# Two bias loads of a mixture-of-experts kernel, moved to GpSimd behind the first weight load

## The chip, the cores and the metric

The kernel runs on one core of one Trainium2 chip. That core has five instruction streams: TensorE (PE in the profile), VectorE (DVE), ScalarE (ACT), GpSimd (POOL) and SyncE (SP). Any of ACT, POOL and SP can issue a DMA; the bytes are moved by the 16 DMA engines of the core. The metric is the device time of one execution in microseconds, lower is better.

## The reference: what is computed

There are 8 experts. Each has its own 256 rows of 512 inputs, a first weight matrix of 512 x 2048, a second of 2048 x 512, and two biases:

```
h   = np.matmul(x, w1) + b1[:, np.newaxis, :]
h   = np.maximum(h, 0)
out = np.matmul(h, w2) + b2[:, np.newaxis, :]
```

Everything comes in and goes out as float32. The inputs are x (8 x 256 x 512), w1 (8 x 512 x 2048), w2 (8 x 2048 x 512), b1 (8 x 2048, that is 64 KB) and b2 (8 x 512, that is 16 KB). Each w1[e] and each w2[e] is 4 MB in HBM.

## The kernel before

The kernel is written by hand for each engine inside one critical section, with semaphores for the order. Weights are cast from float32 to float16 while they are loaded, which only DMAs issued by GpSimd do here, so one GpSimd DMA per matrix brings 4 MB from HBM into 2 MB of SBUF (the last two w2 come in two halves). There are three buffers for w1 and three for w2 (`NW = 3`).

Steps. A loop over s = 0 to 10 runs on every engine (`E + LAG` steps, `LAG = 3`). In step s TensorE does the first layer of expert s (64 matmuls with 128 x 128 weights in 16 groups of four, tile `ph`, line 297) and then the second layer of expert s - 3 (tile `po`, two bias matmuls of line 324 and 32 matmuls of line 314). So steps 0 to 2 have only a first layer, and steps 8 to 10 only a second.

VectorE turns x of the next expert into `xT` by 32 x 32 block transposes (lines 124 and 127) and evicts one half of `po`. ScalarE takes each group of `ph` out of PSUM with the bias b1 and the relu into `hT` (line 231), and evicts the other half of `po` (line 211). There are four PSUM buffers for `ph` (`NPH = 4`): TensorE may be at most four groups ahead of ScalarE, which counts free buffers on the semaphore `s_credit`.

Bias b1. ScalarE needs b1 as one column per group and expert, with the 128 hidden rows on partitions. In the kernel before, b1 is loaded ahead of the section by a DMA of ScalarE (lines 132 and 133) as 32 rows of 2 KB into `b1_rows`; VectorE turns it with four 32 x 512 transposes (line 196) after the x of expert 0, and then raises `s_b1`, for which ScalarE waits once (line 221).

Bias b2. It is loaded by GpSimd right behind the first w1 (line 178), as one row of 4096 numbers cast to float16, in one partition, behind three rows that no result uses. The matmuls of line 324 put it into `po` at the start of each second layer: the weights are a row of ones, the moving operand is 512 numbers at `s * H`.

Order of GpSimd's DMAs (all in one queue, q0): after the semaphore `s_first` (raised by ScalarE's first instruction) come w1 of expert 0, b2, w1 of 1, x of 2 and 3, w1 of 2. From then on each w1 waits until the first layer three experts back is done (`s_ph`, line 154), and each w2 from expert 3 on waits for the second layer three back (`s_po`, line 162). At the end it stores the results of experts 0 to 3 and 4 to 5 (`flush`).

SyncE loads x of experts 0 and 1 (line 135), and then is the gate for TensorE: in each step it waits for `xT` and for the landing of the matrices, and raises `s_go` (lines 246 and 247). In step 0, ahead of these, it waits for b2 (lines 254 and 255). It stores the results of the last two experts.

Of the kernel before, what the change touches and what calls it, by code (L numbers as in the profile page):

```python
# [10 lines left out]
def kernel(  # L11
# [12 lines left out]
    nc = tc.nc  # L24
    fp32 = mybir.dt.float32
    fp16 = mybir.dt.float16
    relu = mybir.ActivationFunctionType.Relu
    PE = mybir.EngineType.PE
    E, T, H = x.shape
    M = w1.shape[2]  # L30
    P = 128
    nTB = T // P
    nKC = H // P
    nJ = M // P
    half = nJ // 2
    TURN = half - 1
    B = 32
    nB = P // B
    LAG = 3
    NW = 3  # L40
    NPH = 4
# [6 lines left out]
    def sbuf(name, shape, dtype):  # L48
        return ctx.enter_context(nc.sbuf_tensor(name, shape, dtype))

    def sem(name):
        return ctx.enter_context(nc.semaphore(name=name))


    ones1 = sbuf("ones1", [1, P], fp16)
    warm = sbuf("warm", [1, P], fp16)
    b2_sb = sbuf("b2_sb", [1, (LAG + E) * H], fp16)
    b1_rows = sbuf("b1_rows", [E * nB, M // nB], fp32)
    b1T = sbuf("b1T", [P, nJ * B + nB - 1], fp32)
    w1_sb = sbuf("w1_sb", [P, NW * nKC * M], fp16)  # L60
    w2_sb = sbuf("w2_sb", [P, NW * nJ * H], fp16)
    xT = sbuf("xT", [P, 2 * nKC * T], fp16)
    hT = sbuf("hT", [P, (LAG + 1) * nJ * T], fp16)
    x32 = [sbuf(f"x32_{e}", [P, nTB, H], fp32) for e in range(2)]
# [19 lines left out]
    landed = {}  # L84

    def load(engine, key, **kw):
        landed[key] = sem(f"d_{key}")
        engine.dma_start(**kw).then_inc(landed[key], 16)  # L88

    s_b1 = sem("b1T")  # L90
# [16 lines left out]
    def transposes(e):  # L107
# [21 lines left out]

    nc.vector.memset(ones1[:], 1.0)  # L130
    tc.keep_in_program_order(nc.scalar.activation(out=warm[:], in_=ones1[:], func=relu).then_inc(s_first, 1))  # L131
    tc.keep_in_program_order(nc.scalar.dma_start(
        out=b1_rows[:], in_=b1.rearrange("e (b i) -> (e b) i", b=nB)))
    for e in range(2):
        tc.keep_in_program_order(nc.sync.dma_start(
            out=x32[e][:], in_=x[e].rearrange("(p tb) h -> p tb h", tb=nTB)))
# [15 lines left out]
    def load_w1(e):  # L152
        if e >= NW:
            nc.gpsimd.wait_ge(s_ph, nJ * (e - NW + 1))
        at = e % NW * nKC * M
        load(nc.gpsimd, f"w1_{e}",
             out=w1_sb[:, at : at + nKC * M].rearrange("p (kc m) -> p kc m", kc=nKC),
             in_=w1[e].rearrange("(p kc) m -> p kc m", kc=nKC))

    def load_w2(e):  # L160
        if e >= NW:
            nc.gpsimd.wait_ge(s_po, nTB * (e - NW + 1))
        dst = w2_sb[:, e % NW * nJ * H : (e % NW + 1) * nJ * H].rearrange("p (j h) -> p j h", j=nJ)
        src = w2[e].rearrange("(p j) h -> p j h", j=nJ)
        cuts = (0, half, nJ) if e in HALVED else (0, nJ)
        for lo, hi in zip(cuts, cuts[1:]):
            load(nc.gpsimd, f"w2_{e}_{lo}", out=dst[:, lo:hi], in_=src[:, lo:hi])

    def flush(first):
        n = GROUPS[first]  # L170
        for tb in range(nTB):
# [3 lines left out]

    nc.gpsimd.wait_ge(s_first, 1)
    load_w1(0)
    load(nc.gpsimd, "b2", out=b2_sb[:, LAG * H :],
         in_=b2.rearrange("e h -> (e h)").rearrange("(o f) -> o f", o=1))
    for s in range(1, E + LAG - 1):  # L180
        if s < E:
            if s in X_LOADS:
                load_x(s)
            load_w1(s)
        if s >= LAG:
            load_w2(s - LAG)
    load_w2(E - 1)
# [4 lines left out]

    nc.vector.sem_inc(s_last, -16 * len(HALVED))
    nc.vector.sem_inc(s_xT, 1)
    for b in range(nB):
        turned = nc.vector.transpose(  # L196
            out=b1T[b * B : (b + 1) * B, nB - 1 - b : nB - 1 - b + nJ * B],
            in_=b1_rows[:].rearrange("r (i j) -> r j i", j=nJ),
        )
    turned.then_inc(s_b1, 1)  # L200

# [16 lines left out]
        if s >= LAG:  # L218
            evict(s - LAG, 1)

    nc.scalar.wait_ge(s_b1, 1)
    for s in range(E + LAG):
        if s < E:
            split = group_of.get(s, (s, 1))[1]
            if s > LAG:
                nc.scalar.wait_ge(s_po, nTB * (s - LAG))
            for j in range(nJ):
                mine = hT[:, s % (LAG + 1) * nJ * T : (s % (LAG + 1) + 1) * nJ * T]
                bias_at = j * B + s * nB + nB - 1
                nc.scalar.wait_ge(s_ph, nJ * s + j + 1)  # L230
                nc.scalar.activation(  # L231
                    out=mine.rearrange("p (tb j k i) -> p j tb k i", tb=nTB, j=nJ, k=split)[:, j],
                    in_=ph[:, j % NPH, 0:T].rearrange("p (tb i k) -> p tb k i", tb=nTB, k=split),
                    func=relu,
                    bias=b1T[:, bias_at : bias_at + 1],
                    scale=1.0,
                ).then_inc(s_credit, 1)
        if s >= LAG:
            evict(s - LAG, 0)
# [5 lines left out]
    def go(key, n=1):  # L245
        nc.sync.wait_ge(landed[key], 16)  # L246
        nc.sync.sem_inc(s_go, n)  # L247

    def store(e, p0, p1, engine):
        dst = out[e].rearrange("(p r) h -> p r h", r=nTB)  # L250
        engine.dma_start(out=dst[p0:p1], in_=results[e][p0:p1]).then_inc(s_last, 16)

    for s in range(E + LAG):
        if s == 0:
            nc.sync.wait_ge(landed["b2"], 16)
        if s < E:
            nc.sync.wait_ge(s_xT, s + 1)
            go(f"w1_{s}")
        e = s - LAG
        if e >= 2:  # L260
            for tb in range(nTB):
                nc.sync.wait_ge(s_out[tb], e - 1)
        if e >= 0 and e not in HALVED:
            go(f"w2_{e}_0", 2)
        elif e == E - 2:
            go(f"w2_{e}_0")
            go(f"w2_{e}_{half}")
        elif e == E - 1:
            go(f"w2_{e}_0")
            for tb in range(nTB):  # L270
                nc.sync.wait_ge(s_out[tb], e)
            store(E - 2, 0, P, nc.sync)
            go(f"w2_{e}_{half}")
# [13 lines left out]
    with nc.Fori(0, E + LAG, 1, engines=[PE]) as s:  # L287
        nc.tensor.wait_ge(s_credit, NPH)
        w_at = at(s % NW * (nKC * M), (NW - 1) * nKC * M)
        with nc.tensor.If(s < E):  # L290
            x_at = at(s % 2 * (nKC * T), nKC * T)
            take(s_go)
            with nc.Fori(w_at, w_at + nJ, half, engines=[PE]) as w_from:
                w_from = w_from.with_bounds(min_val=0, max_val=(NW - 1) * nKC * M + half)
                for j in range(half):
                    for kc in range(nKC):
                        last = nc.tensor.matmul(  # L297
                            ph[:, j % NPH, 0:T],
                            w1_sb[:, bass.ds(w_from + (kc * M + j), P, nJ)],
                            xT[:, bass.ds(x_at + kc * T, T)],  # L300
                            start=(kc == 0),
                            stop=(kc == nKC - 1),
                        )
                        if kc == 0:
                            last.wait_op(s_credit, j + 1, "sem-ge")
                    last.then_inc(s_ph, 1)
                nc.tensor.sem_inc(s_credit, -half)
        with nc.tensor.If(s >= LAG):
            h_at = at((s + 1) % (LAG + 1) * (nJ * T), LAG * nJ * T)
            bank_at = at((s + 1) % 2 * (nTB * H), nTB * H)  # L310
            banks = [po[:, bass.ds(bank_at + tb * H, H)] for tb in range(nTB)]

            def second(tb, h_from, w2_from, j, stop=False):
                return nc.tensor.matmul(  # L314
                    banks[tb],
                    hT[:, bass.ds(h_from + (tb * nJ + j) * P, P)],
                    w2_sb[:, bass.ds(w2_from + j * H, H)],
                    start=False,
                    stop=stop,
                )  # L320

            nc.tensor.wait_ge(s_go, 1)
            for tb in range(nTB):
                nc.tensor.matmul(banks[tb], ones1[:], b2_sb[:, bass.ds(s * H, H)], start=True, stop=False)  # L324
            with nc.Fori(h_at, h_at + 2 * TURN * P, TURN * P, engines=[PE]) as h_from:
                h_from = h_from.with_bounds(min_val=0, max_val=LAG * nJ * T + TURN * P)
                w2_from = at((h_from - h_at) * (H // P) + w_at, ((NW - 1) * nJ + TURN) * H)
                nc.tensor.wait_ge(s_go, 1)
                for tb in range(nTB):
                    for j in range(TURN):  # L330
                        second(tb, h_from, w2_from, j)
                nc.tensor.sem_inc(s_go, -1)
            for tb in range(nTB):
                for j in range(2 * TURN, nJ):
                    last = second(tb, h_at, w_at, j, stop=(j == nJ - 1))
                last.then_inc(s_po, 1)
# [35 lines left out]
```

## Time and profile before

| what | value |
|---|---|
| median of 3 runs | 180.83 us (180.82 to 181.06) |
| the profiled execution itself | 181.16 us |
| its span, first to last instruction | 179.4 us |
| mean granted TensorE clock | 0.969 |
| PE, DVE, ACT, POOL busy | 135.3, 86.8, 75.5, 12.6 us |
| moved by DMA | 40.46 MB as counted by the profile, 226 GB/s |

In the groups of instructions a line shows the source line, the engine, the operation, what is written and from what, the shape, how often, the busy time and the mean duration. "SPq" or "PEq" is the instruction queue (the sequencer) of an engine. "us to landing" of a DMA is the time from its issue until all of its data have arrived. In the rows of the timeline the first number is the start in us, the second how long the group took; in square brackets stands the idle time of the engine ahead of it and what ended it. In the row of the slices each digit is the busy share of one fortieth of the span, in tenths.

### The profile page before, as it was taken

How to read it: one execution, taken by the hardware profiler on the slowest of the kernel's cores; microseconds unless marked ns; L12 is line 12 of the kernel's file. 1: busy time of each engine (PE TensorE's matmuls, PEld its weight loads, DVE VectorE, ACT ScalarE, POOL GpSimd, SP SyncE). 2: the span in 40 equal slices, each digit the busy share in tenths (PEclk: the TensorE clock that was granted, in tenths of full speed). 3: DMA queues.
4: the chain of work that ended last, by engine and by line, in shares of the span. 5: the costliest groups of instructions: out<-in, count | busy, mean ns of one | idle time of the engine just before them, and what ended most of it. 6: DMA issues, size and time to landing. Idle time of an engine off the chain costs nothing. (4 is left out here: it accounts for less than half of the span.)

```text
span 179.4 us, 3015 instructions
## 1 busy us (share of the span) xinstructions
PE 135.3 (75%) x784; PEld 93.1 (52%) x784; DVE 86.8 (48%) x124; ACT 75.5 (42%) x153; POOL 12.6 (7%) x27
## 2 busy tenths in 40 slices
PE   0004978868699890898978896889698896999980
PEld 0003878858689330794468543874298332434330
DVE  1989938576000299998089906992320002030110
ACT  3201686757687113483087506780487211020110
POOL 4200012020200100001010001000200003010000
PEclk9999999999999997599999999999999998799999
DMA  5999999998999999999899999999989999999995
GB/s 214 269 205 206 234 205 206 230 227 186 236 227 190 227 230 216 197 230 227 186 234 230 205 208 230 216 197 230 227 190 230 230 192 217 208 223 212 343 406 248
DMA packets 3826, 40.46 MB, mean 226 GB/s; under 512 B 448, under 2 KB 464, under 8 KB 1136
## 3 DMA queue, kind: packets, MB, share of 16 engines
q0 software_dynamic: 3200, 38.28, 96.6%
q1 hardware_dynamic: 576, 2.10, 3.0%
q10 hardware_dynamic: 48, 0.07, 0.1%
q14 instruction: 2, 0.02, 0.0%
HBM read 71.39 MB, written 4.19 MB: 421 GB/s over the span
## 5 line engine op out<-in xcount | busy, mean ns | idle before, releaser
L297 PE MATMUL ph<-xT,w_sb 128*128 x512 | 72.5, 303 | 33.2 <-PEq L282 30.3
L297 PEld LDWEIGHTS ph<-xT,w_sb 128*128 x512 | 66.6, 146 | 40.1 <-issue 29.3
L231 ACT ACTIVATE hT<-ph,b1T 128x256 f16<-128x256 f32 x128 | 60.1, 474 | 33.7 <-PE ph L297 30.0
L127 DVE STREAM_TRANSPOSE xT<-x 32x256 f16<-32x256 f16 (+1 forms) x64 | 52.7, 892 | 25.3 <-DMA x<-in_x_dram 22.0
L314 PE MATMUL po<-w_sb,hT 128*128 x256 | 58.3, 388 | 1.6 <-issue 1.6
L314 PEld LDWEIGHTS po<-w_sb,hT 128*128 x256 | 25.2, 99 | 33.9 <-issue 8.0
L211 DVE COPY out<-po 32x512 f32<-32x512 f32 (+1 forms) x20 | 13.7, 687 | 44.6 <-PE po L314 44.4
L211 ACT COPY out<-po 32x512 f32<-32x512 f32 (+1 forms) x20 | 11.5, 577 | 47.7 <-PE po L314 47.5
L88 POOL DMA_DIRECT2D w_sb<-in_w_dram x18 | 9.7, 544 | 137.4 <-PE po L314 71.2
L124 DVE STREAM_TRANSPOSE xT<-x 32x256 f16<-32x256 f16 x32 | 14.0, 436 | 0.5
L324 PE MATMUL po<-b_sb,ones 1*128 x16 | 4.8, 379 | 3.9 <-issue 2.5
L211 DVE COPY x<-po 128x512 f32<-128x512 f32 x2 | 1.4, 692 | 13.0 <-PE po L314 13.0
L211 ACT COPY x<-po 128x512 f32<-128x512 f32 x2 | 1.2, 585 | 13.3 <-PE po L314 13.3
L324 PEld LDWEIGHTS po<-b_sb,ones 1*128 1x128 f16 x16 | 1.3, 91 | 6.4 <-issue 6.1
L196 DVE STREAM_TRANSPOSE b1T<-b_rows 32x512 f32<-32x512 f32 x4 | 4.1, 1024 | 0.5 <-issue 0.5
L139 ACT CAST x<-x 128x1024 f16<-128x1024 f32 x1 | 1.0, 1045 | 3.3 <-DMA x<-in_x_dram 3.3
L137 DVE CAST x<-x 128x1024 f16<-128x1024 f32 x1 | 0.7, 724 | 3.1 <-DMA x<-in_x_dram 3.1
L88 POOL DMA_DIRECT2D out_dram<-out x2 | 1.1, 536 | 11.2 <-DVE out L211 11.2
L131 ACT ACT_TABLE_LOAD x1 | 1.3, 1283 | 0.7 <-PEq L356 0.7
L88 POOL DMA_DIRECT2D x<-in_x_dram x2 | 1.2, 608 | 0.0
L130 DVE MEMSET ones<- 1x128 f16 x1 | 0.2, 165 | 0.9 <-PEq L356 0.9
L88 POOL DMA_DIRECT2D b_sb<-in_b_dram x1 | 0.5, 507 | 0.0
(5 smaller groups left out, 0.7 us busy)
## 6 DMA issues: line engine op xcount, KB each, us to landing
w_sb<-in_w_dram POOLq DMA_DIRECT2D x14, 2048.0 KB, 41.2
w_sb<-in_w_dram POOLq DMA_DIRECT2D x4, 1024.0 KB, 22.5
out_dram<-out POOLq DMA_DIRECT2D x1, 2048.0 KB, 25.0
x<-in_x_dram SPq DMA_DIRECT2D x2, 512.0 KB, 3.9
x<-in_x_dram POOLq DMA_DIRECT2D x1, 1024.0 KB, 34.5
out_dram<-out POOLq DMA_DIRECT2D x1, 1024.0 KB, 16.4
out_dram<-x SPq DMA_DIRECT2D x2, 512.0 KB, 6.3
x<-in_x_dram POOLq DMA_DIRECT2D x1, 512.0 KB, 23.1
```

Source lines behind the costliest of these rows:

```text
L88: engine.dma_start(**kw).then_inc(landed[key], 16)
L124: last = nc.vector.transpose(out=dst[:, :, g, :, 0, :], in_=block[:, :, :, 0, :])
L127: last = nc.vector.transpose(out=dst[:, tb, g], in_=block[:, tb])
L131: tc.keep_in_program_order(nc.scalar.activation(out=warm[:], in_=ones1[:], func=relu).then_inc(s_first, 1))
L137: nc.vector.tensor_copy(out=x16[0][0][:], in_=x32[0][:])
L139: tc.keep_in_program_order(nc.scalar.copy(out=x16[1][0][:], in_=x32[1][:]))
L196: turned = nc.vector.transpose(out=b1T[b * B : (b + 1) * B, nB - 1 - b : nB - 1 - b + nJ * B], in_=b1_rows[:].rearrange("r (i j) -> r j i" ...
L211: last = copy(out=results[e][at : at + rows, k * nTB + tb, :], in_=po[k * rows : (k + 1) * rows, bank : bank + H])
L231: nc.scalar.activation(out=mine.rearrange("p (tb j k i) -> p j tb k i", tb=nTB, j=nJ, k=split)[:, j], in_=ph[:, j % NPH, 0:T].rearrange("p ...
L297: last = nc.tensor.matmul(ph[:, j % NPH, 0:T], w1_sb[:, bass.ds(w_from + (kc * M + j), P, nJ)], xT[:, bass.ds(x_at + kc * T, T)], start=(k ...
L314: return nc.tensor.matmul(banks[tb], hT[:, bass.ds(h_from + (tb * nJ + j) * P, P)], w2_sb[:, bass.ds(w2_from + j * H, H)], start=False, st ...
L324: nc.tensor.matmul(banks[tb], ones1[:], b2_sb[:, bass.ds(s * H, H)], start=True, stop=False)
```

## The change

b1 is no longer loaded by ScalarE ahead of the section. GpSimd zeroes a tile `b1_rows` of 32 rows of 2048 numbers, waits for that, and loads b1 into its first eight rows, one row of 8 KB per expert. This stands behind w1 of expert 0 and b2, and ahead of w1 of expert 1. VectorE waits for that load ahead of its four transposes, which have the same shape as before (32 x 512), now from four column ranges of the rows. The columns of `b1T` are arranged anew, and ScalarE waits for the second count of `s_b1`, since the zeroing gives the first.

b2 keeps its place in GpSimd's queue, but lands as eight rows of 512 numbers, each followed by a gap of 32 numbers in SBUF (`B2 = H + B`); the matmuls of line 324 step by `B2`. SyncE waits for b2 in step 3, where the first second layer stands, and not in step 0.

```diff
+    B2 = H + B
...
-    b2_sb = sbuf("b2_sb", [1, (LAG + E) * H], fp16)
-    b1_rows = sbuf("b1_rows", [E * nB, M // nB], fp32)
-    b1T = sbuf("b1T", [P, nJ * B + nB - 1], fp32)
+    b2_sb = sbuf("b2_sb", [1, (LAG + E) * B2], fp16)
+    b1_rows = sbuf("b1_rows", [B, M], fp32)
+    b1T = sbuf("b1T", [P, nJ * B], fp32)
...
-    tc.keep_in_program_order(nc.scalar.dma_start(
-        out=b1_rows[:], in_=b1.rearrange("e (b i) -> (e b) i", b=nB)))
...
     load_w1(0)
-    load(nc.gpsimd, "b2", out=b2_sb[:, LAG * H :],
-         in_=b2.rearrange("e h -> (e h)").rearrange("(o f) -> o f", o=1))
+    load(nc.gpsimd, "b2", out=b2_sb[:, LAG * B2 :].rearrange("o (e h) -> o e h", e=E)[:, :, 0:H],
+         in_=b2.rearrange("(o e) h -> o e h", o=1))
+    nc.gpsimd.memset(b1_rows[:], 0.0).then_inc(s_b1, 1)
+    nc.gpsimd.wait_ge(s_b1, 1)
+    load(nc.gpsimd, "b1", out=b1_rows[0:E], in_=b1)
...
+    nc.vector.wait_ge(landed["b1"], 16)
     for b in range(nB):
         turned = nc.vector.transpose(
-            out=b1T[b * B : (b + 1) * B, nB - 1 - b : nB - 1 - b + nJ * B],
-            in_=b1_rows[:].rearrange("r (i j) -> r j i", j=nJ),
+            out=b1T[b * B : (b + 1) * B],
+            in_=b1_rows[:, b * (M // nB) : (b + 1) * (M // nB)].rearrange("r (i j) -> r j i", j=nJ),
...
-    nc.scalar.wait_ge(s_b1, 1)
+    nc.scalar.wait_ge(s_b1, 2)
...
-                bias_at = j * B + s * nB + nB - 1
+                bias_at = j * B + s
...
-        if s == 0:
+        if s == LAG:
             nc.sync.wait_ge(landed["b2"], 16)
...
-                nc.tensor.matmul(banks[tb], ones1[:], b2_sb[:, bass.ds(s * H, H)], start=True, stop=False)
+                nc.tensor.matmul(banks[tb], ones1[:], b2_sb[:, bass.ds(s * B2, H)], start=True, stop=False)
```

## The prediction

> **What bounds the kernel now.** I read the slices and the DMA queues of the page first.
>
> ```profile
> span 179.4 us, 3015 instructions
> ...
> PEclk9999999999999997599999999999999998799999
> DMA  5999999998999999999899999999989999999995
> ...
> q0 software_dynamic: 3200, 38.28, 96.6%
> q1 hardware_dynamic: 576, 2.10, 3.0%
> q10 hardware_dynamic: 48, 0.07, 0.1%
> ```
>
> The DMA row shows 8 or 9 tenths in all slices but the first and the last, and the queues' shares add up to 99.7% of 16 engines' span. So the 16 DMA engines are full from the start to the end; what counts is how many engine-microseconds are queued, whether they are spread evenly, and whether an engine ever runs dry. q0 are GpSimd's DMAs, q1 SyncE's, q10 the one DMA of ScalarE, which is b1.
>
> Next, the pieces of the chain that ended last (start, duration).
>
> ```profile
> 109.46 39.44 DMA w_sb<-in_w_dram
> ...
> 149.30 0.60 PE po L324 x2
> ...
> 150.15 8.77 PE po L314 x32
> 158.92 0.53 PE po L324 x2
> 159.45 7.01 PE po L314 x32
> 166.46 0.53 PE po L324 x2
> 167.00 7.03 PE po L314 x32
> ...
> 174.05 0.69 DVE x L211
> ```
>
> The end hangs on a w2 that was issued at 109.46 and landed at 148.90: it stood 39 us in the queue. Behind it come three second layers without a break (the first takes 8.77 instead of 7.0 us because the clock row shows a 7 and an 8 there), an eviction and the last store. So two things set the end: when that w2 lands, and the DMA work left behind it.
>
> Third, how deep the queue is: the issues and their time to landing, each from the DMA view of a short window (columns: the tile, queue, count, KB, us to landing), and the timeline of the start. The first fence has, in this order, b1, w1 of expert 0, b2, w1 of 1, x of 2 and 3, w1 of 2, and w1 of 4.
>
> ```profile
> b_rows<-in_b_dram ACTq DMA_DIRECT2D x1, 64.0 KB, 3.4
> ...
> w_sb<-in_w_dram POOLq DMA_DIRECT2D x1, 2048.0 KB, 12.6
> ...
> b_sb<-in_b_dram POOLq DMA_DIRECT2D x1, 8.0 KB, 12.1
> ...
> w_sb<-in_w_dram POOLq DMA_DIRECT2D x1, 2048.0 KB, 21.3
> ...
> x<-in_x_dram POOLq DMA_DIRECT2D x1, 512.0 KB, 23.1
> ...
> w_sb<-in_w_dram POOLq DMA_DIRECT2D x1, 2048.0 KB, 32.5
> ...
> w_sb<-in_w_dram POOLq DMA_DIRECT2D x1, 2048.0 KB, 34.4
> ```
>
> ```profile
> 0.35 0.10 POOL L356 MEMSET const-uint8-127<- 128x1 uint8 x1
> 0.74 1.28 ACT L131 ACT_TABLE_LOAD   x1 [0.74 <-PEq L356]
> ...
> 1.12 0.41 ACTq L132 DMA_DIRECT2D b_rows<-in_b_dram  x1
> 2.03 0.31 ACT L131 ACTIVATE warm<-ones 1x128 f16<-1x128 f16 x1
> 2.65 0.67 POOL L88 DMA_DIRECT2D w_sb<-in_w_dram  x1 [2.21 <-ACT warm L131]
> 3.31 0.51 POOL L88 DMA_DIRECT2D b_sb<-in_b_dram  x1
> 3.80 0.58 POOL L88 DMA_DIRECT2D w_sb<-in_w_dram  x1
> ...
> 4.36 0.66 POOL L88 DMA_DIRECT2D x<-in_x_dram  x1
> ...
> 5.00 0.55 POOL L88 DMA_DIRECT2D w_sb<-in_w_dram  x1
> ...
> 12.60 4.14 DVE L196 STREAM_TRANSPOSE b1T<-b_rows 32x512 f32<-32x512 f32 x4 [0.49 <-issue]
> ...
> 16.08 9.85 PE L297 MATMUL ph<-xT,w_sb 128*128 x64 [16.08 <-PEq L282]
> 16.77 7.20 DVE L124 STREAM_TRANSPOSE xT<-x 32x256 f16<-32x256 f16 x16
> 17.22 0.47 ACT L231 ACTIVATE hT<-ph,b1T 128x256 f16<-128x256 f32 x1 [10.55 <-PE ph L297]
> 18.02 0.47 ACT L231 ACTIVATE hT<-ph,b1T 128x256 f16<-128x256 f32 x1 [0.32 <-PE ph L297]
> ...
> 21.43 5.01 ACT L231 ACTIVATE hT<-ph,b1T 128x256 f16<-128x256 f32 x11 [0.38 <-PE ph L297]
> 26.22 1.07 POOL L88 DMA_DIRECT2D w_sb<-in_w_dram  x2 [20.67 <-PE ph L297]
> ...
> 27.45 4.38 PE L297 MATMUL ph<-xT,w_sb 128*128 x32 [1.52 <-PEq L282]
> ...
> 38.30 4.35 PE L297 MATMUL ph<-xT,w_sb 128*128 x32 [1.56 <-PEq L282]
> ```
>
> Landings: w1 of 0 at 2.65 + 12.6 = 15.25, b2 at 3.31 + 12.1 = 15.4, w1 of 1 at 25.1, x of 2 at 27.5, w1 of 2 at 5.00 + 32.5 = 37.5. When w1 of 3 is issued at 26.22, the engines still have 11 us of work; from there on the queue only gets deeper (the 39 us above).
>
> **The change part by part.**
>
> *b1 out of q10 and into q0.* The bytes stay the same. q10's 0.1% of 179.4 us is about 0.18 us on every engine; finer, q1 spends 3.0% x 179.4 = 5.4 us per engine on 2.10 MB, so 64 KB (0.066 MB) spread over 16 engines cost 0.17 us on each. That leaves the queue ahead of w1 of 0, so w1 can start up to 0.17 us earlier (or not at all earlier, if its own descriptors are late: it is issued only at 2.65). In exchange the same bytes come behind b2. Every DMA of before gave its bytes to all engines as far as the shares show. Eight rows of 8 KB can hardly sit on more than eight engines unless a row is cut. Cut over 16 the net is 0; on eight engines each of those gets 0.34 us, net +0.17, and the other eight -0.17; with w1 starting no earlier, +0.34 and 0. A load has landed only when its slowest engine is done, so what counts is whether the slowest engine is among the eight. Ends: -0.17 and +0.34; I take +0.1, near the middle, since nothing in the page tells the engines apart.
>
> [...] No row of before shows a DMA of eight rows. [...]
>
> *b2 as eight rows.* 8 KB as before, in the same place. Its landing lies 0.16 us behind w1's; if half of the engines carry it, at most another 0.1 us on those. I take 0.
>
> *Zeroing b1_rows, and GpSimd's queue.* 2048 numbers per partition. The trace has no such memset on POOL: the nearest row is 0.10 us for one number. VectorE's transposes take 4.14/4 = 1.03 us for 512 numbers, so 2048 cost 4.1 us at that rate; I take 3 and bound it at 0.1 and 8 (twice that). With the wait and one more issue of 0.51 us, w1 of 1 goes out at 3.80 + 3 + 0.5 = 7.3 instead of 3.80 (bounds 4.4 and 12.3), and x of 2 and w1 of 2 behind it move alike. The engines are busy with w1 of 0 until 15.25, so this is hidden with 3 to 11 us to spare; if that cover were gone, every us of lateness would be a us of the end. Value 0.
>
> *ScalarE without its DMA issue.* 0.41 us at 1.12, under the table load that ends at 2.02; the warm-up activation that frees GpSimd waits for that load. 0.
>
> *SyncE's wait for b2.* In step 0 SyncE waits for b2, `xT` and w1. Without b2, TensorE can start 0.16 us earlier (15.25 against 15.4), at about 15.9. In step 3 the wait falls on a DMA that landed some 30 us before, and nothing queued behind it on SyncE is held. 0 at the end.
>
> *VectorE's and ScalarE's wait for b1.* This is the real move. b1's transposes can begin only when b1 has landed behind w1 of 0 and b2: about 15.4 + 0.4 = 15.8, against 12.60. They end at 15.8 + 4.14 = 19.95, and ScalarE's first activation starts at about 20.2 instead of 17.22. TensorE has four buffers: from 15.9 it does four groups at 0.85 us (the spacing of the activations, 17.22 to 18.02 and on) until 19.3, then stalls until ScalarE has freed one at 20.7. The remaining twelve groups cost 12 x 0.85 = 10.2 us at the slow pace of the start and 12 x 0.45 = 5.4 at the pace behind 21.43 (5.01 us for 11). So the first layer of expert 0 ends between 26.1 and 30.9 instead of 25.93; with about five more slow groups I take 28.5, +2.6 us. Behind it on VectorE, x of expert 1 is turned from 20.0 to 27.2 (7.20 us) instead of until 23.97, which is no later than TensorE is free. Step 1 then starts at about 30.0 instead of 27.45, and steps 1 to 3 are late by some 2.5 us. GpSimd's w1 of 3 goes out near 28.8 (at most 31.2) instead of 26.22, with the engines fed until 37.5. Cover there: 6 us or more.
>
> Where does the lateness end? Here.
>
> ```profile
> 59.78 7.08 PE L314 MATMUL po<-w_sb,hT 128*128 x32 [0.28 <-issue]
> ...
> 72.22 4.03 PE L297 MATMUL ph<-xT,w_sb 128*128 x18 [5.36 <-PEq L282]
> ...
> 37.03 1.07 POOL L88 DMA_DIRECT2D w_sb<-in_w_dram  x2 [9.21 <-PE ph L297]
> ...
> 140.81 7.08 PE L314 MATMUL po<-w_sb,hT 128*128 x32 [0.28 <-issue]
> ```
>
> Before step 4 TensorE idles 5.36 us until w1 of 4 lands (37.03 + 34.4 = 71.4). A lateness of 2.6 us, or of 5.0 at the worst pace, is swallowed there, and from 72 us on TensorE runs as before. Without that gap the 2.6 us would reach the end. Value 0.
>
> [...]
>
> *Sum.* 0.1 + 0 = +0.1 us on the profiled span, 179.5; the profiled execution took 181.16 with 1.8 us around the span, 0.3 above the median. Against the median of 180.83 that gives 180.9 us. I call within 0.2% (0.36 us) the same, which is about what a measurement of this kernel can tell from no change; the three runs spread over 0.24.
>
> **The rivals.**
>
> *b1 sits on few engines* (slower; the other side of my forecast would begin here). If all 64 KB go through one engine, that engine has 16 x 0.17 = 2.7 us more and saves 0.17; every later load waits for it, and the end moves by +2.5: 183.3 us. On four engines it is 4 x 0.17 - 0.17 = +0.5, 181.4. It decides from three engines' worth of crowding on. For it: no row shows how eight rows are dealt out. Against it: b2, one row in one partition, landed only 0.16 us behind w1, so its 16 KB of source were not pulled by one engine alone, which at 2.7 us for 64 KB would take 0.7. 10%.
>
> *The late start is not swallowed* (slower). If ScalarE's first activation came over 8 us later than now, the first layers would be late by more than 5.36 us plus the 1.0 us of waiting that the chain has ahead of 149.30 (the chain's DMA piece ends at 148.90, TensorE was free at 140.81 + 7.08 = 147.89). Each us beyond costs one: a b1 at 25 us, behind w1 of 1, would give about 10 - 6.4 = +3.6, 184.4. For it: VectorE, ScalarE and TensorE all queue behind the one load. Against it: b1 stands ahead of w1 of 1 in its queue. 5%.
>
> *Faster by the tail.* If TensorE's half clock at 151 to 155 does not fall into the first of the three second layers (8.77 against 7.0), they end up to 1.7 us earlier; DMA work then holds the last store, since the DMA row is at 9 until the last slice, so I give it 0.5 of that (ends 0 and 1.7). Together with b1 on engines that are not the last (-0.17) this is -0.6, 180.2 us. For it: the dip follows a short wait, so a small shift of the landing at 148.90 may move it. Against it: nothing in the change moves that wait by more than 0.3 us. 13%.
>
> **How the numbers follow.** Forecast, no change: 72%, with its own range 180.5 to 181.2 (180.83 - 0.33 to + 0.37). Few engines 10%, late start 5%, tail 13%. Slower is 15%, faster 13%, same 72%. The time is the forecast's, 180.9. The range 180.3 to 181.4 takes in the ends -0.17 and +0.34, four engines and the most of the tail's case, and leaves out the crowded engine, the late start and the large gain, under 2 in 10.
>
> **What would show it.** In the changed profile: the DMA row stays at 9 from the second slice on; q10 is gone and q0 has the 0.07 MB; b1 lands within 0.7 us of w1 of 0; line 196 starts near 15.8; the first activation near 20.2; w1 of 3 goes out at 28 to 31; the wait ahead of step 4 shrinks from 5.36 to 1 to 3.5 us, with step 4 still at 72.2 +- 0.3; the w2 of the chain lands at 148.9 +- 0.3. I am wrong if a load after b1 lands 1 us or more later than now with the queue full, or if step 4 starts late, or if the memset holds w1 of 1 beyond 13 us.

## The result, and the profile after

The changed kernel is slower: 181.25 us against 180.86 us (medians of 22 executions each), a ratio of 1.0025 with a 95% interval of 1.0016 to 1.0035, that is +0.45 us (0.29 to 0.63; the two medians themselves lie 0.39 us apart). The forecast was 180.9 us and no change within 0.2%, 180.5 to 181.2; the time lies just above that and in the whole range of 180.3 to 181.4, and the sign that was forecast as likeliest did not come. A second comparison gave 1.0030 (1.0016 to 1.0045).

The profiled executions hide most of this: both have a span of 179.4 us. That of the kernel before is one of its slower ones (181.16 us), that of the changed kernel one of its faster ones (181.15 us). The comparison must go by places in the trace, not by the two spans. First the page of the changed kernel: span, the slices of the DMA engines, the queues.

```profile
span 179.4 us, 3011 instructions
...
DMA  6999999999999999999999999999999999999996
...
q0 software_dynamic: 3232, 38.35, 96.9%
q1 hardware_dynamic: 576, 2.10, 3.0%
q14 instruction: 2, 0.02, 0.0%
```

ScalarE's queue q10 is gone, its 0.07 MB are in q0, and the engines are as full as before. Then the pieces of the chain that ended last (start, duration).

```profile
109.84 39.41 DMA w_sb<-in_w_dram
...
149.65 0.60 PE po L327 x2
...
150.50 8.76 PE po L317 x32
...
159.80 7.01 PE po L317 x32
...
167.34 7.03 PE po L317 x32
...
174.39 0.69 DVE x L214
```

It is the same chain, shifted: the w2 that releases the three last second layers lands at 109.84 + 39.41 = 149.25 instead of 148.90, and each piece behind it is 0.35 us later. So the loss came through the DMA stream. It does not reach the end of this pair of executions: the last stores (first line before, second after) land 6.0 us after their issue instead of 6.3, and both spans come out at 179.4. That these 0.35 us make up the 0.45 of the ratio is therefore argued from their size, and not shown by these two traces.

```profile
out_dram<-x SPq DMA_DIRECT2D x2, 512.0 KB, 6.3
...
out_dram<-x SPq DMA_DIRECT2D x2, 512.0 KB, 6.0
```

The view of DMA issues over short windows shows where it entered (us to landing in the last column; in order w1 of expert 0, b2, b1, w1 of 1).

```profile
w_sb<-in_w_dram POOLq DMA_DIRECT2D x1, 2048.0 KB, 13.3
...
b_sb<-in_b_dram POOLq DMA_DIRECT2D x1, 8.0 KB, 12.9
...
b_rows<-in_b_dram POOLq DMA_DIRECT2D x1, 64.0 KB, 10.7
...
w_sb<-in_w_dram POOLq DMA_DIRECT2D x1, 2048.0 KB, 19.1
```

And the timeline of the changed kernel, its start and step 4.

```profile
2.66 0.67 POOL L89 DMA_DIRECT2D w_sb<-in_w_dram  x1 [2.21 <-ACT warm L132]
3.32 0.53 POOL L89 DMA_DIRECT2D b_sb<-in_b_dram  x1
3.83 1.83 POOL L179 MEMSET b_rows<- 32x2048 f32 x1
3.91 2.31 DVE L136 CAST x<-x 128x1024 f16<-128x1024 f32 x1 [2.82 <-DMA x<-in_x_dram]
...
5.96 0.51 POOL L89 DMA_DIRECT2D b_rows<-in_b_dram  x1 [0.29 <-POOL b_rows L179]
...
6.25 7.18 DVE L125 STREAM_TRANSPOSE xT<-x 32x256 f16<-32x256 f16 x16
6.46 0.57 POOL L89 DMA_DIRECT2D w_sb<-in_w_dram  x1
...
16.63 3.61 PE L300 MATMUL ph<-xT,w_sb 128*128 x16 [16.63 <-PEq L285]
16.66 4.20 DVE L199 STREAM_TRANSPOSE b1T<-b_rows 32x512 f32<-32x512 f32 x4 [3.24 <-DMA b_rows<-in_b_dram]
...
20.90 2.12 ACT L234 ACTIVATE hT<-ph,b1T 128x256 f16<-128x256 f32 x5 [14.68 <-DVE b1T L199]
...
28.86 1.07 POOL L89 DMA_DIRECT2D w_sb<-in_w_dram  x2 [20.77 <-PE ph L300]
...
30.15 9.28 PE L300 MATMUL ph<-xT,w_sb 128*128 x64 [1.58 <-PEq L285]
...
72.60 9.56 PE L300 MATMUL ph<-xT,w_sb 128*128 x64 [3.04 <-PEq L285]
```

w1 of expert 1, the first load behind b1, lands at 6.46 + 19.1 = 25.56 against 25.1: in this trace the whole delay is there from the first load behind b1 on, and does not grow afterwards. (w1 of expert 0 is counted as landed at 2.66 + 13.3 = 15.96 instead of 15.25; by the packet records its last packet ended only 0.15 us later than before, while the completion counts of six engines came 0.7 us late. In the traces of the experiments below it lands at 15.6 to 16.0 us wherever b1 goes into eight or sixteen neighbouring partitions, and at 15.2 to 15.3 with rows four partitions apart or 32 rows, so this lateness goes with the neighbouring partitions. With sixteen rows it costs nothing at the end.) The bias is late as forecast, the first activation at 20.90, and step 1 at 30.15; but the wait ahead of step 4 has shrunk from 5.36 to 3.04 us and swallowed it: step 4 starts at 72.60 instead of 72.22, 0.38 us late, which is the shift of the DMA stream.

### The profile page after: what moved, and what is told of

It reads as the page before. It is cut to its first block, busy times and chain, and to the rows that moved or that the text cites. A ratio compares the mean times of both kernels' runs of the same rounds, so it can differ in the third digit from the quotient of the medians.

```text
span 179.4 us, 3011 instructions
## 1 busy us (share of the span) xinstructions
PE 136.4 (76%) x784; PEld 93.5 (52%) x784; DVE 88.4 (49%) x124; ACT 75.1 (42%) x153; POOL 14.9 (8%) x29
## 5 line engine op out<-in xcount | busy, mean ns | idle before, releaser
L300 PE MATMUL ph<-xT,w_sb 128*128 x512 | 73.6, 307 | 32.4 <-PEq L285 28.8
L214 ACT COPY x<-po 128x512 f32<-128x512 f32 x2 | 1.2, 586 | 13.3 <-PE po L317 13.3
L136 DVE CAST x<-x 128x1024 f16<-128x1024 f32 x1 | 2.3, 2305 | 2.8 <-DMA x<-in_x_dram 2.8
L179 POOL MEMSET b_rows<- 32x2048 f32 x1 | 1.8, 1832 | 0.0
```

Source lines behind the costliest of these rows:

```text
L136: nc.vector.tensor_copy(out=x16[0][0][:], in_=x32[0][:])
L179: nc.gpsimd.memset(b1_rows[:], 0.0).then_inc(s_b1, 1)
L214: last = copy(out=results[e][at : at + rows, k * nTB + tb, :], in_=po[k * rows : (k + 1) * rows, bank : bank + H])
L300: last = nc.tensor.matmul(ph[:, j % NPH, 0:T], w1_sb[:, bass.ds(w_from + (kc * M + j), P, nJ)], xT[:, bass.ds(x_at + kc * T, T)], start=(k ...
```

## The experiments

Three theories stood against each other: A, the DMA side (eight rows on eight engines); B, the late bias that keeps TensorE late; C, GpSimd's zeroing, which holds up VectorE's cast (2.31 us beside it) and, by the theory, the first w1 too. All ratios are to the kernel before, executed beside each kernel on the same chip.

### b2 and SyncE's wait alone

```diff
 # the kernel before, with
+    load(nc.gpsimd, "b2", out=b2_sb[:, LAG * B2 :]....[:, :, 0:H], ...)   # eight rows with gaps
-        if s == 0:
+        if s == LAG:
             nc.sync.wait_ge(landed["b2"], 16)
```

> The kernel before with b2 as eight rows with gaps and SyncE's wait for b2 in step 3; b1 stays as it was. Theory A (the DMA side: b1's 64 KB sit in GpSimd's queue as eight rows on eight engines): within 0.1 us of before, 180.9. Theory B (the late bias keeps TensorE late): b1 is early here, so within 0.1 us of before as well, perhaps 0.1 faster since TensorE starts 0.2 us earlier. Theory C (zeroing on GpSimd collides with VectorE's cast and with the descriptors of the first w1): 0. If this run alone is 0.3 us or more slower, all three fall and the rows of b2 are the cause.

Ratio 1.0009 (1.0000 to 1.0018). An interval of 0 to 0.33 us, so no change that this run can tell from nothing; the moved wait brings nothing at the end, though TensorE starts 0.16 us earlier. Its chain, with the w2 at 148.88 and the first of the last second layers at 7.08 us instead of 8.77 (its page has no dip of the clock there, all slices from 148 to 158 us at 9 tenths):

```profile
109.45 39.43 DMA w_sb<-in_w_dram
...
150.13 7.08 PE po L315 x32
```

### b1 late, but as 32 rows

```diff
 # the kernel of the last run, with
-    tc.keep_in_program_order(nc.scalar.dma_start(out=b1_rows[:], in_=b1....))
+    load(nc.gpsimd, "b1", out=b1_rows[:], in_=b1.rearrange("e (b i) -> (e b) i", b=nB))   # behind b2
+    nc.vector.wait_ge(landed["b1"], 16)
```

> The changed kernel, but b1 in GpSimd's queue as 32 rows of 2 KB like in the kernel before, without zeroing. The bias is as late as in the change (first activation near 20.5 us), only the spread over the engines differs. Theory A: 0 to +0.1 us against before, 180.9, and the w2 of the chain lands at 149.1. Theory B: as slow as the change, +0.4 us, 181.3. Theory C: 0, since nothing is zeroed.

Ratio 1.0000 (0.9992 to 1.0009). The bias is late here as well:

```profile
15.67 4.21 DVE L197 STREAM_TRANSPOSE b1T<-b_rows 32x512 f32<-32x512 f32 x4 [3.69 <-DMA b_rows<-in_b_dram]
...
19.91 2.12 ACT L232 ACTIVATE hT<-ph,b1T 128x256 f16<-128x256 f32 x5 [13.50 <-DVE b1T L197]
...
109.65 39.41 DMA w_sb<-in_w_dram
```

The first activation is 2.7 us late (19.91 against 17.22), and it costs nothing. So B is out at this size of lateness, and so is the move of 64 KB into GpSimd's queue as such. What is left is how the 64 KB are cut, and the zeroing, which this kernel does not have either.

### Zeroing first

```diff
+    nc.gpsimd.memset(b1_rows[:], 0.0).then_inc(s_b1, 1)
     nc.gpsimd.wait_ge(s_first, 1)
     load_w1(0)
...
-    nc.gpsimd.memset(b1_rows[:], 0.0).then_inc(s_b1, 1)
     nc.gpsimd.wait_ge(s_b1, 1)
```

> The changed kernel with the zeroing of b1_rows put ahead of GpSimd's first wait, where GpSimd is idle. VectorE's cast of x should take 0.7 us again instead of 2.3. Theory A: still +0.4 us, 181.3. Theory B: +0.3 to +0.4. Theory C: 0, 180.9, with the first packets of w1 as in the kernel before and w1 of expert 0 landed by 15.5.

Ratio 1.0030 (1.0019 to 1.0041).

```profile
4.07 0.69 DVE L136 CAST x<-x 128x1024 f16<-128x1024 f32 x1 [2.98 <-DMA x<-in_x_dram]
...
109.91 39.42 DMA w_sb<-in_w_dram
```

VectorE's cast is back to 0.69 us from 2.31, so the zeroing did hold it up; the time is not better. C is out: the collision is real and hidden.

### The eight rows in other partitions

```diff
-    load(nc.gpsimd, "b1", out=b1_rows[0:E], in_=b1)
+    load(nc.gpsimd, "b1", out=b1_rows[0 : B : B // E], in_=b1)   # partitions 0, 4, ... 28
-                bias_at = j * B + s
+                bias_at = j * B + s * (B // E)
```

> The changed kernel with b1's eight rows put into partitions 0, 4, 8 to 28 instead of 0 to 7. Still eight rows, so eight engines, and just as late. Theory A in the form that some engines carry more: +0.4 us, 181.3, as the change. Theory A in the form that the eight rows crowd in few neighbouring partitions: +0.1 to +0.2 us, 181.0. Theory B: +0.4. Theory C: +0.4.

Ratio 1.0019 (1.0008 to 1.0030), and together with the zeroing first:

> The run with the zeroing first, and b1's eight rows in partitions 0, 4 to 28. If crowding in neighbouring partitions costs in a single load what it costs in four (a quarter of 1.5 us, 0.35 to 0.4): 0.35 us below the change, +0.1 us against before. If a single load is taken up by buffers and only the eight engines count: within 0.1 us of the change, +0.3 to +0.4.

Ratio 1.0014 (1.0003 to 1.0026). Both are slower than before and both come out below the changed kernel, by 0.06 to 0.16% (0.1 to 0.3 us), but their intervals overlap with its own. So there is a part that stays with eight rows anywhere, and perhaps a part that goes when they stand apart. The bias is less late here than in the change (first activations at 19.84 and 19.85 instead of 20.90), and the cost stays. The chain of the first of the two:

```profile
109.78 39.42 DMA w_sb<-in_w_dram
...
150.45 7.08 PE po L317 x32
```

### Sixteen rows

```diff
 # with the zeroing first
-    load(nc.gpsimd, "b1", out=b1_rows[0:E], in_=b1)
+    load(nc.gpsimd, "b1", out=b1_rows[0:16, 0 : M // 2], in_=b1.rearrange("e (u m) -> (e u) m", u=2))
```

(the columns of `b1T` are arranged to match.)

> The run with the zeroing first, and b1 once as sixteen rows of 4 KB in partitions 0 to 15: all sixteen engines, twice as many partitions. If the engines' number is the cause: 0 to +0.1 us against before, like the 32 rows. If crowding is: +0.1 to +0.2.

Ratio 0.9999 (0.9988 to 1.0011); the w2 lands at 148.84.

```profile
109.45 39.39 DMA w_sb<-in_w_dram
```

All other parts of the change are in this kernel: the zeroing, the late bias, b2's eight rows, the moved wait. The bias is nearly as late as in the change (first activation at 20.51, w1 of 3 out at 29.07 against 28.86), so theory B is out at that size of lateness too. Cutting each row of 8 KB in two brings the time back to that of the kernel before.

### b1 four times

To take the cost of one load out of the spread of the runs, b1 was loaded four times (256 KB in all, no zeroing): as eight rows in neighbouring partitions, as eight rows four partitions apart, and as sixteen rows.

```diff
+    for k in range(4):   # eight rows: partitions 8k to 8k+7
+        load(nc.gpsimd, f"b1_{k}", out=b1_rows[k * E : (k + 1) * E], in_=b1)
 # or: eight rows, partitions k, k+4, ... k+28
+        load(nc.gpsimd, f"b1_{k}", out=b1_rows[k : B : B // E], in_=b1)
 # or: sixteen rows of 4 KB
+        load(nc.gpsimd, f"b1_{k}", out=b1_rows[k % 2 * 16 : k % 2 * 16 + 16, k // 2 * (M // 2) : ...],
+             in_=b1.rearrange("e (u m) -> (e u) m", u=2))
```

> The changed kernel without the zeroing; instead b1 is loaded four times, each time as eight rows of 8 KB, into partitions 0-7, 8-15, 16-23 and 24-31 (256 KB in all). The packets of the changed kernel showed b1's eight rows right behind b2's on the same eight engines. Theory A with the same eight engines each time: 4 x 0.30 = 1.2 us on those, and the end at +1.2 to +1.8 us against before, 182.1 to 182.7. Theory A with the engines taken in turn: 4 x 0.15 = 0.6 us on all, 181.5. Theory of lateness alone: about +0.4, as the change.

> The same four loads of eight rows, but load k goes to partitions k, k+4, k+8 to k+28. Same eight engines each time: as the run with neighbouring partitions, +1.2 us, less what crowding in few partitions costs there. If crowding is the larger part, 0.4 us or more below that run; if the count of engines is all, within 0.15 us of it.

> The same 256 KB, but each of the four loads has sixteen rows of 4 KB, so all sixteen engines have a row. Theory A: the mean work alone, 4 x 0.15 = 0.6 us less what the early start saves (0 to 0.17), so +0.4 to +0.6 us, 181.3 to 181.5, and 0.6 us or more below the run with eight rows. If the count of rows is of no matter: as the run with eight rows.

| b1 loaded four times as | ratio (95%) | us over before |
|---|---|---|
| eight rows, neighbouring partitions | 1.0144 (1.0128 to 1.0159) | 2.6 |
| eight rows, four partitions apart | 1.0066 (1.0052 to 1.0079) | 1.2 |
| sixteen rows | 1.0045 (1.0031 to 1.0058) | 0.8 |

The expectations for neighbouring rows (1.2 to 1.8 us) and for sixteen rows (0.4 to 0.6) were too low, that for rows apart was met at its edge. Crowding in neighbouring partitions costs 1.4 us here and is the larger part. Eight rows apart cost 0.4 us more than sixteen rows, with intervals that overlap a little; this is not the price of eight engines alone, since the sixteen rows stand in neighbouring partitions and crowd too (by the packet records a row of 4 KB takes 0.16 us in the first load and up to 0.38 us in the later ones). In all three kernels b1 is late, most with neighbouring rows (first activation at 23.36), but their DMA rows never fall below 8 tenths between the first slice and the last, so the engines did not run dry. The stretches behind w1 of expert 0 show the crowding (columns: stretch, length, busy time and count of PE, PEld, DVE, ACT, POOL, then clock, DMA share and GB/s), first for neighbouring rows:

```profile
16.50:18.50 2.00, 2.00 (x10) 1.62 (x11) 0.00 (x0) 0.00 (x0) 0.00 (x0) 1.00 0.99 164
18.50:20.00 1.50, 1.50 (x8) 0.88 (x6) 0.81 (x1) 0.00 (x0) 0.00 (x0) 1.00 0.82 175
```

then for the rows four apart:

```profile
16.50:18.50 2.00, 2.00 (x12) 1.58 (x11) 1.99 (x2) 0.00 (x0) 0.00 (x0) 1.00 1.15 246
18.50:20.00 1.50, 1.02 (x5) 0.46 (x3) 1.47 (x3) 0.00 (x0) 0.00 (x0) 1.00 0.92 197
```

The view counts a packet whole in the stretch in which it starts, so a share can exceed 1, and only rate over share can be compared. In the first stretch that is 164/0.99 = 166 GB/s for neighbouring rows against 246/1.15 = 214 for rows apart, in the second 213 and 214: in the first, engines hold packets that cannot get on. The packet records say which (time of one row of 8 KB, by load):

```
rows in neighbouring partitions:  load 1: 0.32 us   loads 2 to 4: 0.68 to 0.92 us
rows four partitions apart:       load 1: 0.32 to 0.35   loads 2 to 4: 0.31 to 0.34
```

The first load of neighbouring rows is taken at full pace; the following ones need up to 0.92 us for eight rows (64 KB), which is 71 GB/s. In a single load, as in the change, the rows themselves look normal (0.32 us), and those that pay are the packets of w1 of expert 1 behind them: those that started in the 2.7 us from 14.6 us on took 0.16 us per engine longer than the usual 1.23 us in the changed kernel, 0.04 to 0.21 us in the three other executions with eight neighbouring rows, and 0 in the runs with rows apart, 16 or 32 rows.

Why rows in neighbouring partitions take longer than rows four apart is not shown by these runs.

### The bias much later

```diff
 # the kernel before, with
     nc.vector.sem_inc(s_xT, 1)
+    nc.vector.wait_ge(landed["w1_1"], 16)
```

> The kernel before, b1 loaded as there, but VectorE waits with the turning of b1 until w1 of expert 1 has landed (25.1 us). ScalarE's first activation then comes at about 29.8 instead of 17.2, 12.6 us late. If lateness up to about 6.4 us is swallowed by the waits ahead of steps 4 to 8 and each us beyond costs one: the first layer of expert 0 ends near 37, w1 of 3 goes out at about 37.3, when the engines have run dry, so +4 to +8 us, 185 to 189. If lateness is swallowed whole by the DMA queue: +2 us at most, from the dry engines alone.

Ratio 1.0195 (1.0175 to 1.0215), 184.2 us or +3.5: between the two guesses. The DMA slices and the timeline:

```profile
DMA  6998999869999999999999999999998999999996
...
25.09 4.13 DVE L197 STREAM_TRANSPOSE b1T<-b_rows 32x512 f32<-32x512 f32 x4 [12.96 <-DMA w_sb<-in_w_dram]
...
29.25 2.11 ACT L232 ACTIVATE hT<-ph,b1T 128x256 f16<-128x256 f32 x5 [22.52 <-DVE b1T L197]
...
37.27 1.06 POOL L88 DMA_DIRECT2D w_sb<-in_w_dram  x2 [31.70 <-PE ph L298]
...
114.37 37.34 DMA w_sb<-in_w_dram
```

The first activation is 12.0 us late. w1 of expert 3 goes out at 37.27, when the queue (empty at 37.5 in the kernel before) has nothing left, and the DMA row dips to 8 and 6 there. The w2 of the chain lands at 151.71, 2.8 us late, so most of the 3.5 us is the dry queue. The rule I had used (each us of lateness beyond 6.4 costs one, which would be 5.6 us) gave too much. The prediction's own figure for such a b1, 184.4 us, is met within 0.2 us, but by luck: it took 10 us of lateness for the 12.0, and its rule did not have the dry queue. How the rest of TensorE's lateness was swallowed in steps 5 to 8 I did not follow further.

### b2 back to one row

The changed kernel once more, and the changed kernel with b2 as one row of 4096 numbers:

```diff
-    B2 = H + B
+    B2 = H
-    load(nc.gpsimd, "b2", out=b2_sb[:, LAG * B2 :]....[:, :, 0:H], in_=b2.rearrange("(o e) h -> o e h", o=1))
+    load(nc.gpsimd, "b2", out=b2_sb[:, LAG * H :], in_=b2.rearrange("e h -> (e h)").rearrange("(o f) -> o f", o=1))
```

> The changed kernel itself, beside the three below on one chip. +0.3 to +0.6 us against before, as measured first (1.0025). All theories agree.

> The changed kernel with b2 as one row of 4096 numbers as before, so that b2's 8 KB go over sixteen engines again and b1's rows stay as in the change. If b2's rows add to the load of the same eight engines: 0.04 to 0.1 us below the change. If b2 decides which eight engines b1 gets, and these matter: different by up to 0.3 us either way.

Ratios 1.0030 (1.0016 to 1.0045) and 1.0024 (1.0010 to 1.0037): not told apart. b2's shape makes no difference that these runs can show.

The w2 of the chain in the change once more, with b2 as one row, and in the run with the zeroing first and the rows apart:

```profile
109.81 39.41 DMA w_sb<-in_w_dram
...
109.99 39.44 DMA w_sb<-in_w_dram
...
109.69 39.55 DMA w_sb<-in_w_dram
```

So over all traces with b1 loaded once and turned as soon as it is there, this landing parts the kernels: 148.84 to 149.06 us in the four without eight rows of b1 (the kernel before, b2's rows alone, 32 rows, sixteen rows), 149.20 to 149.43 in the six with them. The four without them cost nothing that the runs can tell, the six with them cost 0.25 us or more by their ratios.

## Why the prediction was right or wrong

**What bounds the kernel: right.** The DMA stream; the chain after is that of before, moved as a whole by 0.35 us when the w2 lands later. The two signs given for it, step 4 at 72.2 and the w2 at 148.9, each +- 0.3, were both missed by a little: 72.60 and 149.25.

**b1 into q0: the right step, mis-sized.** This is the term of the sum that decided. I took +0.1 us between -0.17 and +0.34; the whole change measured +0.45 (0.29 to 0.63), and with sixteen rows in place of eight nothing is left of it (0.9999). Three parts were off. First, the saving of 0.17 us from b1's absence at the start did not come. In the packet records:

```
first packet of w1 of expert 0, mean over 16 engines:    before      change
  starts at (us)                                          4.94        4.69
  takes longer than the usual 1.23 us by (us)             0.03        0.24
```

It starts 0.25 us earlier and takes 0.21 us longer. Why it does so was not tried; with the zeroing first it is the same (0.30 us longer), and in none of the eight traces with b1 loaded once from GpSimd is more than 0.08 us left of the earlier start. Second, choosing a value near the middle because "nothing in the page tells the engines apart" was the error: with 0.3 us more on eight of sixteen engines, one of those eight is likely the slowest of all, and the upper case, the +0.34, was the one to take. By the packet records b2's eight rows and b1's eight rows go to the same eight engines (each b1 row starts 0.08 us behind a b2 row, eight times of eight), which then carry 0.31 us for b1 and 0.04 us more for b2 than before (0.101 against 0.065). Less the 0.04 us that were saved, that is +0.31 us; the two runs with the rows apart show 0.25 and 0.34 us. Third, crowding in neighbouring partitions wasn't in the sum at all. In one load it is worth 0.1 to 0.3 us by the difference of the medians, which the intervals do not separate from nothing; in four loads it is clear.

The packet records also show which engine is last. On each of b1's eight engines the first packet of w1 of 1 starts 5 or 6 ns behind the end of a b1 row, so the eight can be told from the others and followed. Their lag to each other then hardly changes, but for two packets of q14, the queue that the page names instruction (8 KB and 0.32 us each, at 33.4 and 48.9 us in the changed kernel): at these moments one engine falls back by 0.53 and one by 0.32 us. For the same packet of the stream near 139 us, the last engine starts at 139.26 us in the changed kernel against 138.91 before, the 0.35 us of the chain. In all six traces with b1 once as eight rows that last engine is one of the eight. The eight also fall back by a further 0.08 to 0.11 us in the mean between 16 and 139 us, about as much as both packets make if they fall on the eight ((0.53 + 0.32) / 8 = 0.11). With the rows apart this matters: the last engine is only 0.11 and 0.04 us later than before at 23 us, and 0.31 and 0.34 us later at 139 us. Why these packets meet b1's engines, and what eight rows would cost if they met the others, is open.

How eight rows are dealt out, which no row of before showed, the packets of the changed kernel do: eight packets of 8 KB, 0.32 us each, one per engine. So it is the prediction's case of eight engines that came.

**b2 as eight rows: 0, right as far as the runs can tell.** 1.0009 (1.0000 to 1.0018) alone, and no difference within the change.

**Zeroing: right at the end, its side effect not seen.** It took 1.83 us where I took 3 (bounds 0.1 and 8), and w1 of 1 went out at 6.46 instead of the 7.3 I gave. That VectorE's cast beside it would take 2.31 instead of 0.72 us I had not in the list; it moved the end of expert 0's x to 6.25 + 7.18 = 13.4, still ahead of w1, so the cover held. In the run with the zeroing first the cast takes 0.69 us.

**SyncE's wait and ScalarE's DMA issue: 0, right.** TensorE in fact started later (16.63 instead of 16.08), since w1 of expert 0 was counted as landed later; it was of no matter.

**The late bias: right.** Forecast first activation 20.2, measured 20.90; w1 of 3 out at 28.8, measured 28.86; step 1 at 30.0, measured 30.15; the wait ahead of step 4 at 1 to 3.5 us, measured 3.04. The runs with 32 and with sixteen rows show that it costs nothing.

**The rivals.** Few engines: the rival had the mechanism that decides, but put its threshold at three engines' worth of crowding; eight engines were enough. (By its own sum its four engines give 181.3 us, not 181.4.) Late start: not in the change, and in the run made for it smaller than by my rule. The tail: the dip of TensorE's clock in the first of the last second layers (0.50 granted from 152 to 154 us, before as after) comes and goes among the traces (the layer takes 7.08 us in six of them, 8.71 to 8.77 in the kernel before, the change and six others), so it is not tied to this change; the execution with the rows four apart had no dip and took 181.18 us, the profiled one of the change had it and took 181.15. A gain of 1.7 us there is not a gain at the end.

**What stays open.** The executions of the changed kernel spread more (180.98 to 181.98 us) than those of the kernel before (180.64 to 181.09 but for one of 181.6). In the second comparison the two overlap more (180.97 to 182.06 against 180.64 to 181.73). What makes that spread was not found. The trace of the changed kernel is of an execution below its median (181.15 against 181.25), that of the kernel before of one above (181.16 against 180.86), so how the 0.35 us of shift become the 0.45 us of the ratio is not shown.

## What to carry to other kernels

In a kernel whose DMA engines are full from start to end, a small load can cost what it adds to its busiest engine, as here, where the last engine stayed 0.35 us late up to the w2 of the chain: cut it into sixteen or 32 rows, even if the rows get shorter (sixteen of 4 KB or 32 of 2 KB cost nothing here, eight of 8 KB cost 0.45 us). Rows that go into neighbouring partitions at the same time can crowd (here up to 0.92 us for a row of 8 KB, against 0.31 to 0.34 four partitions apart), and the load behind them may be the one that shows it (0.04 to 0.21 us per engine on w1 of expert 1). Where the ends of a term are an even spread and an uneven one, take the uneven one: here the slowest engine decided (+0.31 us on b1's eight), not the mean.

## What the runs showed of the hardware that was not expected

- Two DMAs of eight rows, one right behind the other on GpSimd's queue, went to the same eight of sixteen engines (each b1 row starts 0.08 us behind a b2 row). Four loads of eight rows of b1, four partitions apart, cost 1.2 us, about four times the 0.31 us of one row.
- 64 KB into eight neighbouring partitions, behind another such load, took up to 0.92 us (71 GB/s); into eight partitions four apart 0.31 to 0.34 us (211 GB/s at 0.31).
- A VectorE cast of 128 x 1024 took 2.31 us beside a GpSimd zeroing of 1.83 us, and 0.69 us without.
- The first packets of a load that found the engines free 0.25 us earlier took 0.21 us longer, so that 0.04 us was won.
- What one engine is behind the others at 16 us it is still behind at 139 us, 0.37 and 0.47 us in the mean of b1's eight engines, with the engines full all the time.
